# Gathered rows used one per tick at a group's end, with a sum over partitions moved among the last tiles

## Chip, cores and metric

The kernel runs on 1 core of one Trainium2 chip. The metric is the device time of one execution in microseconds (us); the kernel before takes 3470.04 us, the median of 3 runs (3468.87 to 3470.82).

## What is computed

One residual block on 512 tokens of width 2048 in fp32: a gated merge of forgetting attention and multi-scale pooling, and then PEER, a retrieval of experts of one neuron each. The change lies in the last part:

```python
q = (xt @ w_query)                                  # 8 heads
top 16 of 256 candidates per head -> expert_idx, gates = softmax(top_s)
def token_block(args):
    xb, idx, g = args
    u = jnp.take(expert_u, idx, axis=0)             # 128 rows of 2048 per token
    a = jnp.einsum('thkd,td->thk', u, xb)
    hid = jax.nn.gelu(a) * g
    vsel = jnp.take(expert_v, idx, axis=0)
    return jnp.einsum('thk,thkd->td', hid, vsel)
x = x + peer(rms_norm(x, norm2_g), ...)
```

## The kernel before, in words

The 512 tokens are treated in three parts. The first 128 (group 0 of the rows) and the last 64 (group 1 of the rows) fetch the rows of their experts, as the reference does. The 320 in the middle are multiplied with all 16384 experts, of which most get a gate of zero.

**Gathered rows.** A list `items` holds 128 fetches of `u` rows and 128 of `v` rows for group 0, then 64 and 64 for group 1, whose 64 tokens are spread over two partitions each (`GQ` = 2), so that the two halves have to be added in the end. A fetch (`row_load`, L787) is an indirect DMA of POOL's queue that brings one row of 2048 to each of 128 partitions, 1 MB, into one of two, later three buffers (`row`, `xrow`). Its use (`row_use`) is one instruction of VectorE (DVE): a dot product with `tok`, the tokens, for `u` (L824), and a multiply-add into `tok`, now the sum, for `v` (L827). Rows are doled out by `tick`, which stands in the middle of every tile of the products: first `run_gens` takes each generator of `gens` one step on, then `rows(rate)` adds `rate` to a credit (3 at most) and for every whole credit uses the oldest row and fetches another. While `hold` is set, a row that would have to be used waits. When all rows of a group are fetched, the last line of `rows` uses all that are still in the buffers, in that same tick. The use of the last `u` row starts `to_v`: it loads the tokens into `tok` once more (SP's queue), takes the Gelu on ScalarE (ACT) and one tick later multiplies with the gates and, for group 1, masks `tok`. The use of the last `v` row starts `to_next`: for group 0 it stores `tok` as `yg`, and then `tok_u` loads and scales the tokens of group 1.

**The joint stage.** The dense tokens go through 32 groups of 512 experts. In the first 16 only `u` is multiplied, and the result goes to memory; the other 16, the joint stage from about 2090 us on, have twelve tiles each: four U tiles (`u_tile`, 48 matmuls into `psm`) and eight V tiles (48 matmuls into `psv`, `s` = 0 to 7). Each weight tile is loaded by SP's queue (`wraw`, `xraw`, L152), rounded to a high half `whi` by ACT (L162), and the low half `wlo` is made by VectorE (L174), two pieces each, up to two tiles ahead; a matmul is done as three with high and low halves. `h_make` (L1440 to L1443) gates the activations of a U tile, `at`, or of a stored one, `sp`, and splits them into `h5h` and `h5l`, which the V tiles multiply. After a V tile VectorE adds `psv` to `acc` (L1498). Each of the 192 tiles holds one tick, with a `rate` of the rows left over 184. POOL, ACT, SP and VectorE take their instructions in the order in which the program issues them.

**The end.** After the last V tile, rows that are left are used; a 128 x 64 matrix `sel` of zeros and ones is built (L1508 to L1513), four matmuls with it add the two halves of each of the last 64 tokens (L1517), ACT copies each out of PSUM (L1518), and SP stores the result as `yg2` (L1519).

```python
    def rows(rate):
        ...
        if row["n"] == len(items) or items[row["n"]][0] != row["grp"]:
            while row["live"] and not row["hold"]:
                row_use()
```

Of the kernel before, what the change touches and what calls it, by code (L numbers as in the profile page):

```python
# [12 lines left out]
F32 = mybir.dt.float32  # L13
F32R = mybir.dt.float32r
I32 = mybir.dt.int32
# [3 lines left out]
OP = mybir.AluOpType  # L19
AX = mybir.AxisListType  # L20

P = 128
S = 512
# [11 lines left out]
NG = NB - ND  # L35
GQ = P // NG
# [26 lines left out]
def block_kernel(ctx, tc, a):  # L63
    nc = tc.nc
# [5 lines left out]
    prow = ctx.enter_context(tc.tile_pool(name="prow", bufs=1))  # L70
# [71 lines left out]
    def row_tile():  # L142
        extra["row"] += 1
        if extra["rows"] is not None and extra["row"] % 3 == 0:
            return extra["rows"].tile([P, D], F32, name="xrow")
        return prow.tile([P, D], F32, name="row", bufs=2)
# [55 lines left out]
    gens = []  # L202

    def run_gens():
        for g in list(gens):
            try:
                next(g)
            except StopIteration:
                gens.remove(g)
# [52 lines left out]
    def acc_bank():  # L262
        return psm.tile([P, S], F32, name="psm")
# [83 lines left out]
    for c in range(4):  # L347
        x4 = xA[:, 4 * c:4 * c + 4, :]
        nc.vector.tensor_tensor(x4, x4, g1[:, 4 * c:4 * c + 4, None].to_broadcast([P, 4, NA]),
                                op=OP.mult)  # L350
# [207 lines left out]
    for n, (kind, i) in enumerate(groups_a):  # L558
        ps = acc_bank()
# [127 lines left out]
    for i in range(4):  # L687
        ps = acc_bank() if i else first_o
# [11 lines left out]
    tok = prow.tile([P, D], F32, name="tok")  # L700
# [76 lines left out]
    row = dict(n=0, credit=0.0, live=[], hold=0, on=False, ready=0, grp=0)  # L777
# [21 lines left out]

    def to_v(grp, n):  # L800
        row["hold"] = 1
        src = x2t_d if grp == 0 else x2g_d.rearrange("t q d -> (t q) d")
        nc.sync.dma_start(tok, src)
        nc.scalar.activation(gact[:, :n], gact[:, :n], AF.Gelu_apprx_tanh)
        yield
        nc.vector.tensor_tensor(gact[:, :n], gact[:, :n], ggat[grp], op=OP.mult)
        if grp:
            nc.vector.tensor_scalar(tok, tok, qmask[:, 0:1], None, op0=OP.mult)
        row["hold"] = 0

    def to_next(grp):
        row["hold"] = 1
        if grp == 0:
            nc.sync.dma_start(a["yg"], tok)
            yield
            yield from tok_u(x2g_d.rearrange("t q d -> (t q) d"), rg[:, 0:1])
            row["hold"] = 0
            row["grp"] = 1
        yield

    def row_use():
        grp, kind, j, n, r = row["live"].pop(0)
        if kind == "u":
            nc.vector.scalar_tensor_tensor(r, r, 1.0, tok, op0=OP.mult, op1=OP.mult,  # L824
                                           accum_out=gact[:, j:j + 1])
        else:
            nc.vector.scalar_tensor_tensor(tok, r, gact[:, j:j + 1], tok, op0=OP.mult, op1=OP.add)  # L827
        if j == n - 1:
            gens.append(to_v(grp, n) if kind == "u" else to_next(grp))
            run_gens_last()  # L830

    def depth():
        return 2 if extra["rows"] is None else 3

    def rows(rate):
        if not row["on"]:
            return
        row["credit"] = min(row["credit"] + rate, 3.0)
        while row["credit"] >= 1.0 and row["n"] < len(items) and items[row["n"]][0] == row["grp"] \
                and row["grp"] < row["ready"]:  # L840
            if len(row["live"]) >= depth():
                if row["hold"]:
                    return
                row_use()
            if len(row["live"]) < depth():
                row_load()
            row["credit"] -= 1.0
        if row["n"] == len(items) or items[row["n"]][0] != row["grp"]:
            while row["live"] and not row["hold"]:
                row_use()  # L850

    def tick(rate):
        run_gens()
        rows(rate)
# [36 lines left out]
    for i in range(4):  # L891
        kk = p3.tile([P, 2, 2 * P], F32, name="kk", bufs=2)
        nc.gpsimd.dma_start(kk, a["keys"][2 * i:2 * i + 2].rearrange("h p i k -> p h (i k)"))
        ps = acc_bank()
# [166 lines left out]
    for n, (kind, i) in enumerate(order_b):  # L1061
        if n == len(order_b) - 7:
            extra["raws"] = extra["rows"] = None
        ps = acc_bank()
# [4 lines left out]
        elif kind == "pin":  # L1069
# [3 lines left out]
            if i == 7:  # L1073
                ps = acc_bank()
# [33 lines left out]
    for c in (2, 3, 0, 1):  # L1108
        rv = p2.tile([P, 4, NB], F32, name="apr", bufs=1)
        nc.sync.dma_start(rv, ap_d[c])  # L1110
        for j in range(4):
# [3 lines left out]
                                    op=OP.subtract)  # L1115
# [52 lines left out]
    for dt in range(KD):  # L1168
# [5 lines left out]
        ps = acc_bank()  # L1174
# [95 lines left out]
    for h in range(H):  # L1270
# [3 lines left out]
        for half in range(2):  # L1274
            if h == 0 and half == 0:
                ps = first_q
            else:
                ps = acc_bank()
# [167 lines left out]
    def h_later(hps, n, at, gt, i):  # L1446
        hps[n] = h_make(at, gt, i)
        yield

    left_rows = len(items) - row["n"]  # L1450
    ticks = 12 * (NIG - LAG)
    rate = left_rows / (ticks - 8)
    sps = {}

    def spilled(g, i):
# [10 lines left out]
    for g in range(LAG):  # L1466
# [11 lines left out]
        for s in range(8):  # L1478
# [8 lines left out]
            ps = psv.tile([P, 2, S], F32, name="psv")  # L1487
# [14 lines left out]
    while row["live"] or row["n"] < len(items):  # L1502
        run_gens()
        rows(2.0)
    run_gens()

    sel = prow.tile([P, NG], F32, name="selg")
    si = prow.tile([P, NG], I32, name="selgi")  # L1508
    nc.gpsimd.iota(si, pattern=[[-GQ, NG]], base=0, channel_multiplier=1)
    nc.vector.tensor_scalar(sel, si, 0.0, None, op0=OP.is_ge)  # L1510
    sel2 = prow.tile([P, NG], F32, name="selg2")
    nc.vector.tensor_scalar(sel2, si, float(GQ), None, op0=OP.is_lt)
    nc.vector.tensor_tensor(sel, sel, sel2, op=OP.mult)  # L1513
    out = row_tile()
    for c in range(4):
        ps = acc_bank()
        nc.tensor.matmul(ps[:NG], lhsT=sel, rhs=tok[:, c * S:(c + 1) * S], start=True, stop=True)  # L1517
        nc.scalar.copy(out[:NG, c * S:(c + 1) * S], ps[:NG])  # L1518
    nc.sync.dma_start(a["yg2"], out[:NG])  # L1519
    es_v.close()  # L1520
    es_7.close()
    es_6.close()
# [74 lines left out]
```

## Time and profile before

| what | value |
|---|---|
| median of 3 runs | 3470.04 us |
| the profiled execution, its time | 3467.64 us |
| its span, first to last instruction | 3465.8 us |
| busy: TensorE (PE), VectorE (DVE), ScalarE (ACT), GpSimd (POOL) | 96%, 77%, 44%, 19% |
| mean granted clock of TensorE | 0.985 |
| bytes moved | 1036.90 MB, 299 GB/s on the mean |

The busy share of TensorE comes from modelled ends of pipelined matmuls, so the waits and the granted clock say more than it does. Waits are given as the instruction that waited, what it waited for, the sum in us, the number of waits and the longest. In a timeline the first column is the start in us from the span's start, the second the length in us; what stands in brackets at the end is the idle time ahead and what ended it. The granted clock is a share of 2.4 GHz.

### The profile page before, as it was taken

What the parts mean: (1) busy time and instruction counts of PE and PEld (TensorE: products, weight loads), DVE (VectorE), ACT (ScalarE), POOL (GpSimd) and SP (SyncE); (2) the same over time, 40 slices, a digit from 0 to 9 for tenths busy, and PEclk for the clock granted to TensorE, in tenths of its full rate; (3) what the DMA queues carried; (4) which work ended last, traced back from release to release, by engine and by line L of the source; (5) the groups of instructions that cost most, each with busy time, mean ns of one, the idle gap of its engine ahead of it and who ended that gap; (6) DMA issues with size and microseconds to landing.
All of it is one profiled execution on the core that took longest, in us unless ns stands there. A gap on an engine that the chain in (4) does not pass through costs nothing.

```text
span 3465.8 us, 50471 instructions
## 1 busy us (share of the span) xinstructions
PE 3334.0 (96%) x20236; PEld 3155.4 (91%) x20236; DVE 2685.1 (77%) x3482; ACT 1515.4 (44%) x2263; POOL 652.4 (19%) x411
## 2 busy tenths in 40 slices
PE   7999899999998999999999989999999999999998
PEld 5656599999998999999999989999999999999997
DVE  5556787787876876887778758888887888888885
ACT  5655434545443333346476753333333333333332
POOL 0000012233321221310000002222222222222221
PEclk9999999999998999999999999999999999999999
DMA  7898867787877897864555689999998999899994
GB/s 263 305 360 313 312 239 272 268 312 268 309 288 283 319 362 278 312 229 161 201 189 193 215 305 345 357 355 351 350 347 338 359 354 354 338 358 353 340 357 151
DMA packets 226762, 1036.90 MB, mean 299 GB/s; under 512 B 21344, under 2 KB 107536, under 8 KB 112928
## 3 DMA queue, kind: packets, MB, share of 16 engines
q1 hardware_dynamic: 144640, 574.14, 44.4%
q0 software_dynamic: 56480, 406.96, 31.5%
q10 hardware_dynamic: 25408, 52.59, 3.9%
q8 instruction: 158, 2.59, 0.3%
q14 instruction: 76, 0.62, 0.0%
HBM read 980.05 MB, written 53.56 MB: 298 GB/s over the span
## 4 chain that ended last, share of the span: by engine, by line
PE 55%; DVE 14%; issue 12%; DMA 8%; ACT 7%; POOL 2%; ACTq 0%; SPq 0%; POOLq 0%; DVEq 0%
PE psm L223 9%; PE psm L221 9%; PE psm L222 9%; PE psv L222 6%; PE psv L223 6%; PE psv L221 6%; PE psm L240 6%; DVE wlo L174 5%; DMA row<-v,gidx 3%; ACT whi L162 3%; ACT o L1385 2%; DVE tok L827 1%; POOL row L787 1%; PE psx L222 1%; PE psx L223 1%
## 5 line engine op out<-in xcount | busy, mean ns | idle before, releaser
L174 DVE TENSOR_TENSOR wlo<-wraw,whi 128x1024 fp32r<-128x1024 f32 x728 | 869.2, 1220 | 294.9 <-ACT whi L162 291.6
L162 ACT CAST whi<-wraw 128x1024 fp32r<-128x1024 f32 x728 | 753.5, 1047 | 658.0 <-PE psv L222 375.9
L223 PE MATMUL psv<-h5h,wlo 128*128 128x320 f32 x2048 | 636.1, 311 | 14.3 <-DVE wlo L174 14.3
L221 PE MATMUL psm<-xnh,whi 128*128 128x320 f32 x2048 | 637.4, 311 | 10.3 <-ACT at L1410 9.8
L221 PE MATMUL psv<-h5h,whi 128*128 128x320 f32 x2048 | 636.7, 311 | 6.6 <-ACT h5h L1442 6.4
L223 PE MATMUL psm<-xnh,wlo 128*128 128x320 f32 x2048 | 634.3, 310 | 6.7 <-DVE wlo L174 6.6
L222 PE MATMUL psv<-h5l,whi 128*128 128x320 f32 x2048 | 637.4, 311 | 1.1
L222 PE MATMUL psm<-xnl,whi 128*128 128x320 f32 x2048 | 633.8, 309 | 0.0
L787 POOL DMA_INDIRECT row<-v,gidx x139 | 219.1, 1576 | 1136.4 <-DVE tok L827 1090.1
L223 PEld LDWEIGHTS psv<-h5h,wlo 128*128 128x128 f32 x2048 | 386.9, 189 | 15.3 <-DVE wlo L174 15.3
L221 PEld LDWEIGHTS psm<-xnh,whi 128*128 128x128 f32 x2048 | 386.5, 189 | 10.8 <-ACT at L1410 10.0
L221 PEld LDWEIGHTS psv<-h5h,whi 128*128 128x128 f32 x2048 | 387.0, 189 | 8.8 <-ACT h5h L1442 8.8
L223 PEld LDWEIGHTS psm<-xnh,wlo 128*128 128x128 f32 x2048 | 386.3, 189 | 8.1 <-DVE wlo L174 8.1
L222 PEld LDWEIGHTS psv<-h5l,whi 128*128 128x128 f32 x2048 | 386.9, 189 | 4.9 <-DVE h5l L1443 4.6
L222 PEld LDWEIGHTS psm<-xnl,whi 128*128 128x128 f32 x2048 | 386.5, 189 | 0.0
L221 PE MATMUL psm<-hh,whi 128*128 128x384 f32 x1024 | 353.6, 345 | 0.0
L787 POOL DMA_INDIRECT row<-u,gidx x135 | 223.8, 1658 | 660.1 <-DVE row L824 567.2
L222 PE MATMUL psm<-hl,whi 128*128 128x384 f32 x1024 | 346.4, 338 | 0.0
L223 PE MATMUL psm<-hh,wlo 128*128 128x384 f32 x1024 | 346.4, 338 | 0.0
L827 DVE SCALAR_TENSOR_TENSOR tok<-row,gact,tok 128x2048 f32<-128x2048 f32 x139 | 326.0, 2345 | 19.1 <-DMA row<-v,gidx 18.0
L824 DVE SCALAR_TENSOR_TENSOR row<-row,tok 128x2048 f32<-128x2048 f32 x135 | 307.4, 2284 | 9.1 <-DMA row<-u,gidx 9.0
L162 ACT CAST whi<-xraw 128x1024 fp32r<-128x1024 f32 x148 | 153.5, 1046 | 182.2 <-PE psv L222 145.7
(393 smaller groups left out, 5183.4 us busy)
## 6 DMA issues: line engine op xcount, KB each, us to landing
wraw<-uT SPq DMA_DIRECT2D x112, 1024.0 KB, 6.7
wraw<-vd SPq DMA_DIRECT2D x96, 1024.0 KB, 7.4
wraw<-w1A SPq DMA_DIRECT2D x48, 1024.0 KB, 6.7
xraw<-vd SPq DMA_DIRECT2D x32, 1024.0 KB, 9.4
wraw<-wgl SPq DMA_DIRECT2D x23, 1024.0 KB, 8.4
g_d<-stg ACTq DMA_DIRECT2D x10, 2048.0 KB, 10.9
gt<-g_d SPq DMA_DIRECT2D x32, 640.0 KB, 10.3
xraw<-w1A SPq DMA_DIRECT2D x16, 1024.0 KB, 7.3
```

The source lines that it names most:

```text
L162: nc.scalar.copy(hi, raws[i][:, half * HD:(half + 1) * HD])
L174: nc.vector.tensor_tensor(lo, raws[i][:, half * HD:(half + 1) * HD], hi.bitcast(F32), op=OP.subtract)
L221: nc.tensor.matmul(ps, lhsT=wh, rhs=xh, start=first and i == 0, stop=False)
L222: nc.tensor.matmul(ps, lhsT=wh, rhs=xl, start=False, stop=False)
L223: nc.tensor.matmul(ps, lhsT=wl, rhs=xh, start=False, stop=last and i == n - 1)
L240: nc.tensor.matmul(ps, lhsT=xs[:, k, :], rhs=ws, start=first and kk == 0 and n == 0, stop=last and kk == 3 and n == len(terms) - 1)
L787: nc.gpsimd.indirect_dma_start(out=r, out_offset=None, in_=a[kind], in_offset=bass.IndirectOffsetOnAxis(ap=gidx[grp][:, j:j + 1], axis=0))
L824: nc.vector.scalar_tensor_tensor(r, r, 1.0, tok, op0=OP.mult, op1=OP.mult, accum_out=gact[:, j:j + 1])
L827: nc.vector.scalar_tensor_tensor(tok, r, gact[:, j:j + 1], tok, op0=OP.mult, op1=OP.add)
L1385: nc.scalar.activation(o2[:, j, :], o2[:, j, :], AF.Copy, scale=idT[2][:, 4 * q + j:4 * q + j + 1])
```

## The change

Four things change. At the end of a group at most one row is used per tick, and none in a tick that has used one already (`used`). What follows a group's last use starts one tick later (`yield` after `hold` is set), and for group 0 the next `tok` is loaded another tick later. The sum over partitions goes into `to_next`, which spreads its four matmuls and copies over ticks of the last V tiles; its matrix is built ahead of the joint stage. The rate is the rows left over 180 ticks, in place of 184.

```diff
     def to_v(grp, n):
         row["hold"] = 1
+        yield
         src = x2t_d if grp == 0 else x2g_d.rearrange("t q d -> (t q) d")
         nc.sync.dma_start(tok, src)
         nc.scalar.activation(gact[:, :n], gact[:, :n], AF.Gelu_apprx_tanh)
...
     def to_next(grp):
         row["hold"] = 1
+        yield
         if grp == 0:
             nc.sync.dma_start(a["yg"], tok)
+            yield
             yield
             yield from tok_u(x2g_d.rearrange("t q d -> (t q) d"), rg[:, 0:1])
             row["hold"] = 0
             row["grp"] = 1
-        yield
+        else:
+
+            out = row_tile()
+            for c in range(4):
+                ps = acc_bank()
+                nc.tensor.matmul(ps[:NG], lhsT=selg[0], rhs=tok[:, c * S:(c + 1) * S],
+                                 start=True, stop=True)
+                yield
+                nc.scalar.copy(out[:NG, c * S:(c + 1) * S], ps[:NG])
+            nc.sync.dma_start(a["yg2"], out[:NG])
...
         row["credit"] = min(row["credit"] + rate, 3.0)
+        used = False
...
                 row_use()
+                used = True
...
         if row["n"] == len(items) or items[row["n"]][0] != row["grp"]:
-            while row["live"] and not row["hold"]:
+            if row["live"] and not row["hold"] and not used:
                 row_use()
...
     left_rows = len(items) - row["n"]
     ticks = 12 * (NIG - LAG)
-    rate = left_rows / (ticks - 8)
+    rate = left_rows / (ticks - 12)
...
     while row["live"] or row["n"] < len(items):
         run_gens()
         rows(2.0)
-    run_gens()
-
-    sel = prow.tile([P, NG], F32, name="selg")
...
-    out = row_tile()
-    for c in range(4):
-        ps = acc_bank()
-        nc.tensor.matmul(ps[:NG], lhsT=sel, rhs=tok[:, c * S:(c + 1) * S], start=True, stop=True)
-        nc.scalar.copy(out[:NG, c * S:(c + 1) * S], ps[:NG])
-    nc.sync.dma_start(a["yg2"], out[:NG])
+    while gens:
+        run_gens()
```

The six instructions that build `sel` stand unchanged ahead of `left_rows` now. Line numbers of the changed kernel differ: a use of a `u` row is L838, of a `v` row L841, the accumulation L1523.

Where the instructions move, on VectorE at the last V tiles of group 15. A row use is `tok<-row,gact,tok`, or with `xrow`. Before:

```order
L174 TENSOR_TENSOR wlo<-wraw,whi 128x1024 x2
L827 SCALAR_TENSOR_TENSOR tok<-row,gact,tok 128x2048
L827 SCALAR_TENSOR_TENSOR tok<-xrow,gact,tok 128x2048
L827 SCALAR_TENSOR_TENSOR tok<-row,gact,tok 128x2048 x2
L1498 TENSOR_TENSOR acc<-acc,psv 128x640
L174 TENSOR_TENSOR wlo<-wraw,whi 128x1024 x2
L1498 TENSOR_TENSOR acc<-acc,psv 128x640
L174 TENSOR_TENSOR wlo<-xraw,whi 128x1024 x2
L1498 TENSOR_TENSOR acc<-acc,psv 128x640
L174 TENSOR_TENSOR wlo<-wraw,whi 128x1024 x2
```

and with the change:

```order
L174 TENSOR_TENSOR wlo<-wraw,whi 128x1024 x2
L841 SCALAR_TENSOR_TENSOR tok<-row,gact,tok 128x2048
L1523 TENSOR_TENSOR acc<-acc,psv 128x640
L174 TENSOR_TENSOR wlo<-wraw,whi 128x1024 x2
L841 SCALAR_TENSOR_TENSOR tok<-row,gact,tok 128x2048
L1523 TENSOR_TENSOR acc<-acc,psv 128x640
L174 TENSOR_TENSOR wlo<-xraw,whi 128x1024 x2
L841 SCALAR_TENSOR_TENSOR tok<-xrow,gact,tok 128x2048
L1523 TENSOR_TENSOR acc<-acc,psv 128x640
L174 TENSOR_TENSOR wlo<-wraw,whi 128x1024 x2
L841 SCALAR_TENSOR_TENSOR tok<-row,gact,tok 128x2048
L1523 TENSOR_TENSOR acc<-acc,psv 128x640
```

The four uses in one tick are one use in each of the first five V tiles.

On SP's queue, where the rows of group 0 have ended, in group 6; `yg<-tok` is the store of the sum, `tok<-x2g_d` the load that overwrites it, `xrow<-g2r` the factors. Before:

```order
L152 DMA wraw<-vd 128x2048
L814 DMA yg<-tok 128x2048
L1434 DMA gt<-g_d 128x10x128
L152 DMA wraw<-vd 128x2048
L793 DMA tok<-x2g_d 128x2048
L795 DMA xrow<-g2r 128x2048
L1457 DMA sp<-a_d 128x320
L152 DMA xraw<-vd 128x2048
```

and with the change:

```order
L152 DMA wraw<-vd 128x2048
L1482 DMA sp<-a_d 128x320
L152 DMA xraw<-vd 128x2048
L816 DMA yg<-tok 128x2048
L1482 DMA sp<-a_d 128x320
L152 DMA wraw<-uT 128x2048
L1482 DMA sp<-a_d 128x320
L152 DMA wraw<-uT 128x2048
L793 DMA tok<-x2g_d 128x2048
L795 DMA xrow<-g2r 128x2048
```

The store and the loads stand later, behind other weight loads, and further from each other.

On VectorE in group 11, where the `u` rows of group 1 have ended; `gact<-gact,ggat` and `tok<-tok,qmask` are the gates and the mask of `to_v`. Before:

```order
L824 SCALAR_TENSOR_TENSOR row,gact<-row,tok 128x2048
L174 TENSOR_TENSOR wlo<-wraw,whi 128x1024 x2
L806 TENSOR_TENSOR gact<-gact,ggat_2302 128x64
L808 TENSOR_SCALAR tok<-tok,qmask 128x2048
L1440 TENSOR_TENSOR at<-at,gt 128x320
L1443 TENSOR_TENSOR h5l<-at,h5h 128x320
L1440 TENSOR_TENSOR sp<-sp,gt 128x320
L1443 TENSOR_TENSOR h5l<-sp,h5h 128x320
L827 SCALAR_TENSOR_TENSOR tok<-row,gact,tok 128x2048
L1440 TENSOR_TENSOR at<-at,gt 128x320
```

and with the change:

```order
L838 SCALAR_TENSOR_TENSOR row,gact<-row,tok 128x2048
L1523 TENSOR_TENSOR acc<-acc,psv 128x640
L174 TENSOR_TENSOR wlo<-wraw,whi 128x1024 x2
L1523 TENSOR_TENSOR acc<-acc,psv 128x640
L174 TENSOR_TENSOR wlo<-xraw,whi 128x1024 x2
L807 TENSOR_TENSOR gact<-gact,ggat_2302 128x64
L809 TENSOR_SCALAR tok<-tok,qmask 128x2048
L841 SCALAR_TENSOR_TENSOR tok<-row,gact,tok 128x2048
L841 SCALAR_TENSOR_TENSOR tok<-xrow,gact,tok 128x2048
L841 SCALAR_TENSOR_TENSOR tok<-row,gact,tok 128x2048
L1523 TENSOR_TENSOR acc<-acc,psv 128x640
L174 TENSOR_TENSOR wlo<-wraw,whi 128x1024 x2
```

The last use of a `u` row, the gates and the mask have moved from U tiles to V tiles; one tick without a row use stands between, and three uses follow the mask at once.

## Rows read from the trace of the kernel before

**Rows 1.** Waits of PE, whole run: line <- waited for: us, times, longest.

```profile
PE psv L223 <- DVE wlo L174: 14.3, 4, 7.9
```

**Rows 2.** Waits of PE at 2640:2690, 2690:3020, 3020:3060 and 3390:3415, in this order.

```profile
PE psv L223 <- DVE wlo L174: 6.4, 3, 5.0
...
PE psv L221 <- ACT h5h L1442: 0.3, 1, 0.3
...
PE psv L221 <- ACT h5h L1442: 2.7, 1, 2.7
...
PE psv L223 <- DVE wlo L174: 7.9, 1, 7.9
```

**Rows 3.** DVE timeline (start, us, ...): accumulations behind V tile 7, groups 0, 5, 6, 10, 11, 14, 15.

```profile
2156.70 0.82 DVE L1498 TENSOR_TENSOR acc<-acc,psv 128x640 f32<-128x640 f32 x1 [1.69 <-PE psv L223]
...
2581.28 0.82 DVE L1498 TENSOR_TENSOR acc<-acc,psv 128x640 f32<-128x640 f32 x1 [1.69 <-PE psv L223]
...
2676.09 0.81 DVE L1498 TENSOR_TENSOR acc<-acc,psv 128x640 f32<-128x640 f32 x1
...
3014.44 0.82 DVE L1498 TENSOR_TENSOR acc<-acc,psv 128x640 f32<-128x640 f32 x1 [1.74 <-PE psv L223]
...
3104.84 0.82 DVE L1498 TENSOR_TENSOR acc<-acc,psv 128x640 f32<-128x640 f32 x1 [1.69 <-PE psv L223]
...
3359.66 0.82 DVE L1498 TENSOR_TENSOR acc<-acc,psv 128x640 f32<-128x640 f32 x1 [1.08 <-PE psv L223]
...
3454.76 0.82 DVE L1498 TENSOR_TENSOR acc<-acc,psv 128x640 f32<-128x640 f32 x1 [6.22 <-PE psv L223]
```

**Rows 4.** Windows: us, busy and count by engine (PE PEld DVE ACT POOL), PEclk, DMA, GB/s.

```profile
2640.00:2650.00 10.00, 7.04 (x36) 7.05 (x37) 7.04 (x7) 0.00 (x0) 3.41 (x2) 0.67 0.82 292
3411.00:3415.00 4.00, 4.00 (x17) 4.00 (x18) 3.81 (x4) 0.00 (x0) 0.00 (x0) 0.54 0.99 341
```

**Rows 5.** DVE timeline, group 15: first and last of four row uses, and the low halves.

```profile
3395.88 2.34 DVE L827 SCALAR_TENSOR_TENSOR tok<-row,gact,tok 128x2048 f32<-128x2048 f32 x1
...
3406.46 2.35 DVE L827 SCALAR_TENSOR_TENSOR tok<-row,gact,tok 128x2048 f32<-128x2048 f32 x1 [3.45 <-DMA row<-v,gidx]
...
3409.46 2.35 DVE L174 TENSOR_TENSOR wlo<-wraw,whi 128x1024 fp32r<-128x1024 f32 x2
```

**Rows 6.** Timeline, group 6: SP's V weight behind the store of tok, and DVE's low halves.

```profile
2641.98 5.62 SPq L152 DMA_DIRECT2D wraw<-vd  x1
...
2658.41 2.36 DVE L174 TENSOR_TENSOR wlo<-wraw,whi 128x1024 fp32r<-128x1024 f32 x2 [5.92 <-ACT whi L162]
```

**Rows 7.** Timeline, group 11: ACT's Gelu of the rows, and DVE's mask.

```profile
3038.16 0.26 ACT L804 ACTIVATE gact<-gact 128x64 f32<-128x64 f32 x1 [2.77 <-DVE row L824]
...
3042.87 1.29 DVE L808 TENSOR_SCALAR tok<-tok,qmask 128x2048 f32<-128x2048 f32 x1 [0.85 <-DMA tok<-x2g_d]
```

**Rows 8.** Timeline of the end: an accumulation, the sum over partitions, its copies, the store.

```profile
3447.71 0.82 DVE L1498 TENSOR_TENSOR acc<-acc,psv 128x640 f32<-128x640 f32 x1 [3.95 <-PE psv L223]
...
3456.09 3.67 PE L1517 MATMUL psm<-tok,selg 128*64 128x512 f32 x8 [1.38 <-DVE selg L1513]
...
3457.20 0.58 ACT L1518 COPY xrow<-psm 64x512 f32<-64x512 f32 x1 [15.63 <-PE psm L1517]
...
3459.80 0.58 ACT L1518 COPY xrow<-psm 64x512 f32<-64x512 f32 x1 [0.28 <-PE psm L1517]
...
3460.41 0.55 SPq L1519 DMA_DIRECT2D yg<-xrow  x1
```

**Rows 9.** DVE timeline: first use of a v row, and the joint stage's start.

```profile
1359.38 2.35 DVE L827 SCALAR_TENSOR_TENSOR tok<-row,gact,tok 128x2048 f32<-128x2048 f32 x1 [7.17 <-DMA row<-v,gidx]
...
2078.71 2.50 DVE L174 TENSOR_TENSOR wlo<-wraw,whi 128x1024 fp32r<-128x1024 f32 x2 [13.58 <-ACT whi L162]
```

**Rows 10.** GB/s in 40 slices of the span (page, part 2), and the window 2670:2680.

```profile
GB/s 263 305 360 313 312 239 272 268 312 268 309 288 283 319 362 278 312 229 161 201 189 193 215 305 345 357 355 351 350 347 338 359 354 354 338 358 353 340 357 151
...
2670.00:2680.00 10.00, 10.00 (x70) 10.00 (x70) 9.57 (x11) 2.77 (x5) 1.88 (x2) 1.00 1.01 418
```

More of the change, by code (lines that the diff above doesn't have):

```diff
@@ L818, in to_next @@
             row["grp"] = 1
-        yield
+        else:
[7 more added lines that the diff above has]
+            nc.sync.dma_start(a["yg2"], out[:NG])
+    selg = []
     def row_use():
@@ L1448, in h_later @@
         yield
+    sel = prow.tile([P, NG], F32, name="selg")
+    si = prow.tile([P, NG], I32, name="selgi")
+    nc.gpsimd.iota(si, pattern=[[-GQ, NG]], base=0, channel_multiplier=1)
+    nc.vector.tensor_scalar(sel, si, 0.0, None, op0=OP.is_ge)
+    sel2 = prow.tile([P, NG], F32, name="selg2")
+    nc.vector.tensor_scalar(sel2, si, float(GQ), None, op0=OP.is_lt)
+    nc.vector.tensor_tensor(sel, sel, sel2, op=OP.mult)
+    selg.append(sel)
     left_rows = len(items) - row["n"]
     ticks = 12 * (NIG - LAG)
-    rate = left_rows / (ticks - 8)
+    rate = left_rows / (ticks - 12)
     sps = {}
@@ L1504, in block_kernel @@
         rows(2.0)
-    run_gens()
-    sel = prow.tile([P, NG], F32, name="selg")
[L1508 to L1513, printed above, removed]
-    out = row_tile()
-    for c in range(4):
-        ps = acc_bank()
-        nc.tensor.matmul(ps[:NG], lhsT=sel, rhs=tok[:, c * S:(c + 1) * S], start=True, stop=True)
-        nc.scalar.copy(out[:NG, c * S:(c + 1) * S], ps[:NG])
-    nc.sync.dma_start(a["yg2"], out[:NG])
+    while gens:
+        run_gens()
     es_v.close()
```

## Prediction

> **What bounds the kernel now.** I read the waits of TensorE first, then the starts of one VectorE line to see which stretches are longer than their like, then the instructions around each long stretch, and last the tail and the transfer rates.
>
> The reader is to see that in the joint stage (16 groups of four U tiles and eight V tiles) TensorE is the bound, and that it is let down at a few places only. Over the whole run it waits 14.3 us for the low halves of V tiles (`psv` for `wlo`), in four waits [rows 1]; 6.4 us of them lie at 2640 to 2690 us, 7.9 at 3390 to 3415, and at 3020 to 3060 there are 2.7 us more for `h5h` [rows 2]. These are the places where gathered rows change group or kind, or run out: group 6 (rows of the first 128 tokens end), group 11 (`u` to `v` rows of the last 64), group 15 (the end).
>
> A wait costs more than itself. The starts of the accumulation behind V tile 7 show it [rows 3]: five undisturbed groups take (2581.28 - 2156.70)/5 = 84.92 us each. Group 6 takes 94.81 (9.89 over), group 11 90.40 (5.48 over), group 15 95.10 (10.18 over): 25.55 us in all, against some 17 us of listed waits. Part of the rest is the clock: after TensorE has idled for the 7.9 us its granted clock is 0.54 in the next 4 us, and it is 0.67 at 2640 to 2650, so mostly at 1.2 GHz in the one and part of the time in the other, against 2.4 GHz else [rows 4].
>
> The causes stand in the same stretches. In group 15 four row uses are issued in one tick; they start at 3395.88, the last waits 3.45 us for its row and starts at 3406.46, and only behind it come the accumulation and the low halves at 3409.46, which TensorE has been waiting for [rows 5]. In group 6 the same happens, and the store of `tok`, issued in that tick, stands on SP's queue ahead of weight loads until the last use is done: the next V weight is issued at 2641.98 (its issue alone spans 5.62 us), and `wlo` at 2658.41 has waited 5.92 us for `whi` [rows 6]. In group 11 ACT's Gelu, issued in the tick of the last `u` use, holds ACT for 2.77 us, then the mask waits 0.85 us for `tok` [rows 7].
>
> **The change, part by part.** The sum is made against the profiled execution, 3467.64 us; the median of the runs, 3470.04, is 2.40 above it, which I add at the end.
>
> *One row per tick at a group's end, the follow-up a tick later.* Group 6: after the change this group has no tick with more than two row uses in the order, the store of `tok` goes out one tick after its last use (so SP never waits there) and the next `tok` two ticks on. The product that opens the next rows falls alone in a tick of the next group's U tiles. VectorE then has less per tick than in any undisturbed tick, so I take the whole excess as gained: 9.89 us; bounds 0 and 9.89. Group 15: one use in each of V tiles 0 to 4, none waiting for a fresh fetch, since three buffers at one use per 7.05 us tick leave some 21 us for a fetch that took under 11 here (it could go out only behind the use of 3395.88, and was there at 3406.46): 10.18 us gained; bounds 5 and 10.18.
>
> Group 11: Gelu and the mask move into V tiles. What is late next is one tick with the mask and three row uses, 1.29 + 3 x 2.35 = 8.34 us on VectorE [rows 5, 7]. Queued behind it are the accumulation and the low halves of the tile after next. Where VectorE has caught up, which the empty tick ahead of it gives, a V tile's start is followed by the accumulation (0.82) and two halves (2.35), then the burst, then accumulation and the first half of the tile after next: 3.17 + 8.34 + 0.82 + 1.18 = 13.5 us, against two tiles of 7.05 (3447.71 to 3454.76) on TensorE, 14.1 [rows 3, 5, 8]. It fits by 0.6 us if `tok` has landed; the wait seen now, 0.85, would use that up. I take 0.5 us lost of the 5.48 gained; bounds: nothing lost, or all 5.48 lost again.
>
> *The higher rate* (rows left over 180 ticks in place of 184). By the order the pairs (two uses in a tick) are 42 in place of 40, and come on the fourth U tile in seven groups (0 to 2, 12 to 15) in place of four. That is the worst place: `h5h` of that tile is needed in the next tile. Group 0 is the same before and after; of the other three pairs in that place one costs TensorE 0.3 us and two nothing [rows 2]. Three more at 0.3: 0.9 us lost; bounds 0 and 3 x 2.35 = 7.
>
> *The sum over partitions among the last V tiles.* Each of the four products with its pieces takes (3459.80 - 3457.20)/3 = 0.87 us on TensorE [rows 8]. Three now stand between V tiles, on the path: 2.6 us lost. They wait for nothing: `tok` is final a tick earlier, and the copies on ACT, 0.58 us each, lie in its idle time. The tail gets shorter. Now from the last accumulation (3454.76) to the issue of the last store (3460.41) it is 5.65 us; after, one product (3456.09 to 3457.20, 1.11) and one copy with the way to SP's issue (3459.80 to 3460.41, 0.61) are left, 1.7 us: 3.9 us gained; bounds 3 and 4.1. Store and end behind it stay.
>
> *The selection matrix, built early.* Three instructions of VectorE and one of POOL go to the start of the joint stage, into 13.58 us in which VectorE waits anyway [rows 9]: nothing. If POOL, whose row fetch stands ahead, came late there, it would cost what this cover can't hold, some 1 us.
>
> *The change from `u` to `v` rows of the first tokens.* VectorE waits 7.17 us for a row at 1359 [rows 9], and TensorE for nothing in that stretch. Nothing, within plus or minus 4 us.
>
> Sum: -25.55 + 0.5 + 0.9 + 2.6 - 3.9 = -25.45 us; 3467.64 - 25.45 = 3442.2; with the 2.40 of the median **3444.6 us**, 0.73% faster. About 0.2% (6.9 us) is what a measurement of this kernel can tell from no change.
>
> **Rivals.** *A new wait in place of the old ones.* If the burst in group 11 costs all of its 5.48 again and the pairs their 7, of which I have counted 0.5 and 0.9, 11 us go: 3455.7. For it: VectorE has no idle tick around U tiles. Against it: pairs have cost 0.3 so far.
>
> *The transfers bound it.* A shorter stage moves the same rows in less time. Slices 26 to 30 of the span, groups without a long wait, move 347 to 357 GB/s, 352 on the mean [rows 10]; rows, about half of these bytes (some 15 of 1 MB a group beside 12 weight tiles of that size), at a 2% higher rate ask for some 356. If 352 were the limit, a group would take 1.1% longer, 0.97 us, over 15 groups 14.5: 3459. If 347 were, 2.6%, 2.2 us a group, 33 us: 3478. Against it: 418 GB/s were moved at 2670 to 2680 [rows 10], and no row is waited for between the places named. The Trainium skill (DMA: Bandwidth & Descriptors, "Where 436 GB/s comes from") puts what HBM gives one core at about 358 GB/s and says that this side binds loads from HBM. By that limit 356 would pass with almost nothing to spare, and the catch-up after a pause would not, so it speaks for this rival; the 418 measured here goes against it.
>
> *Slower: VectorE becomes the bound in U tiles.* Fourteen groups have a pair in a U tile after the change. If each made TensorE wait its 2.35 us and lose 2 us to the clock besides (half of the 4 us stretch of [rows 4]), 14 x 4.35 = 61 us: 3505. It decides from 2.4 us per pair on: 14 x 2.4 = 33, the gain and 6.9 more. Against it: the order before has thirteen such pairs, and outside groups 0 and 11 they show 0.3 us in all.
>
> *The change doesn't do what it says*: the waits only move by a tick, since a fetch still comes late. Then groups 6 and 15 keep their excess, and only group 11, the pairs and the tail are left: 3470.04 - 4.98 + 0.9 - 1.3 = 3464.7, no change. Against it stand the empty ticks in the order.
>
> **How the numbers follow.** Forecast 0.78; new wait 0.10; transfers 0.05 (0.02 faster, 0.02 no change, 0.01 slower); no effect 0.04; VectorE bound 0.03. Faster 0.78 + 0.10 + 0.02 = 0.90, the same 0.02 + 0.04 = 0.06, slower 0.01 + 0.03 = 0.04. The range takes in the bounds around the forecast (nothing lost at the burst and pairs, 4 us at the first change of rows: 3439) and the first rival: **3438 to 3457 us**.
>
> **What would show it.** Right: no wait of TensorE for `wlo` over 1 us after 2600 us; groups 6 and 11 at 84.9 to 86 us, group 15 at 87.5; the granted clock at 1.00 through the last three; four products of `tok`, three of them between V tiles; last store under 2 us after the last accumulation. Wrong: a wait of several us behind the burst in group 11, waits for `h5h` in groups 1, 2 and 12 to 15, or row uses that wait for their fetches in mid-group.

## The result, and the profile after

The changed kernel takes 3448.68 us (median of 6 runs, 3445.58 to 3456.2), the kernel before 3469.56 (6 runs beside them, 3468.15 to 3470.86): ratio 0.9943, 95% interval 0.9931 to 0.9955. The forecast was 3444.6, its range 3438 to 3457. The profiled execution took 3448.07 us, with a span of 3446.3.

TensorE's waits from the joint stage on come first. For its products all of 2120 to 3480 us lists one wait, at 3072 us, in group 11 (the waits of its weight loads have a list of their own, which comes up at e_urate):

```profile
PE psv L223 <- DVE wlo L174: 1.3, 1, 1.3
```

The waits of groups 6 and 15 [rows 2] are gone. The accumulations behind V tile 7 of groups 0, 5, 6, 10, 11, 14 and 15 answer to [rows 3] (VectorE's timeline: start, duration, instruction, idle time before it):

```profile
2161.62 0.81 DVE L1523 TENSOR_TENSOR acc<-acc,psv 128x640 f32<-128x640 f32 x1
...
2584.93 0.82 DVE L1523 TENSOR_TENSOR acc<-acc,psv 128x640 f32<-128x640 f32 x1 [1.69 <-PE psv L223]
...
2669.47 0.82 DVE L1523 TENSOR_TENSOR acc<-acc,psv 128x640 f32<-128x640 f32 x1 [3.95 <-PE psv L223]
...
3008.50 0.82 DVE L1523 TENSOR_TENSOR acc<-acc,psv 128x640 f32<-128x640 f32 x1 [1.74 <-PE psv L223]
...
3095.57 0.81 DVE L1523 TENSOR_TENSOR acc<-acc,psv 128x640 f32<-128x640 f32 x1
...
3351.11 0.81 DVE L1523 TENSOR_TENSOR acc<-acc,psv 128x640 f32<-128x640 f32 x1
3414.55 0.82 DVE L1523 TENSOR_TENSOR acc<-acc,psv 128x640 f32<-128x640 f32 x1 [1.69 <-PE psv L223]
3422.78 0.82 DVE L1523 TENSOR_TENSOR acc<-acc,psv 128x640 f32<-128x640 f32 x1 [5.14 <-PE psv L223]
...
3439.25 0.82 DVE L1523 TENSOR_TENSOR acc<-acc,psv 128x640 f32<-128x640 f32 x1 [7.41 <-PE psv L223]
```

From the two traces the whole span is accounted for:

| stretch (us) | before | after | foretold | measured |
|---|---|---|---|---|
| up to group 0's last accumulation | 2156.70 | 2161.62 | 0 (±4) | +4.92 |
| group 6 | 94.81 | 84.54 | -9.89 | -10.27 |
| group 11 | 90.40 | 87.07 | -4.98 | -3.33 |
| group 15, three products in it | 95.10 | 88.14 | -7.58 | -6.96 |
| the twelve other groups | 1017.75 | 1017.88 | +0.9 | +0.13 |
| last accumulation to the end of the span | 11.04 | 7.05 | -3.9 | -3.99 |
| span | 3465.8 | 3446.3 | -25.45 | -19.5 |

Below the first line it is -24.42, one us from the sum. Two lines need an explanation: group 11 still takes more than its neighbours, and each V tile with a product takes 3422.78 - 3414.55 = 8.23 us where one without takes 7.04.

In group 11 the burst of mask and three uses runs as foretold (VectorE; below it POOL's issues of the rows that refill the three buffers):

```profile
3054.26 1.28 DVE L809 TENSOR_SCALAR tok<-tok,qmask 128x2048 f32<-128x2048 f32 x1
3055.57 2.35 DVE L841 SCALAR_TENSOR_TENSOR tok<-row,gact,tok 128x2048 f32<-128x2048 f32 x1
...
3060.35 2.35 DVE L841 SCALAR_TENSOR_TENSOR tok<-row,gact,tok 128x2048 f32<-128x2048 f32 x1
...
3069.55 2.35 DVE L841 SCALAR_TENSOR_TENSOR tok<-row,gact,tok 128x2048 f32<-128x2048 f32 x1 [3.85 <-DMA row<-v,gidx]
```

```profile
3058.19 2.93 POOL L787 DMA_INDIRECT row<-v,gidx  x1 [10.29 <-DVE tok L841]
3061.43 2.08 POOL L787 DMA_INDIRECT xrow<-v,gidx  x1 [0.30 <-issue]
3063.82 1.56 POOL L787 DMA_INDIRECT row<-v,gidx  x1 [0.30 <-issue]
```

What waits is not the burst but the use a tick later: three uses in one tick empty all three buffers, so the next row, asked for at 3058.19, is not there until 3069.55, 11.4 us later. An accumulation and the next low halves stand behind that use. The tail answers to [rows 8]: ACT's last copy and SP's store.

```profile
3440.25 0.58 ACT L830 COPY xrow<-psm 64x512 f32<-64x512 f32 x1 [4.13 <-PE psm L827]
...
3440.86 0.55 SPq L831 DMA_DIRECT2D yg<-xrow  x1
```

The store is issued 1.6 us after the last accumulation starts, 5.65 before.

### The profile page after: what moved, and what is told of

The parts are those of the page before. It is cut to its first block, busy times and chain, and to the rows that moved or that the text cites. A ratio compares the mean times of both kernels' runs of the same rounds, so it can differ in the third digit from the quotient of the medians.

```text
span 3446.3 us, 50478 instructions
## 1 busy us (share of the span) xinstructions
PE 3331.0 (97%) x20236; PEld 3151.2 (91%) x20236; DVE 2684.6 (78%) x3482; ACT 1516.3 (44%) x2263; POOL 659.1 (19%) x411
## 4 chain that ended last, share of the span: by engine, by line
PE 58%; DVE 17%; issue 8%; DMA 8%; ACT 7%; POOL 1%; ACTq 0%; SPq 0%; DVEq 0%; POOLq 0%
PE psm L223 9%; PE psm L222 9%; PE psm L221 9%; PE psv L222 6%; PE psv L223 6%; PE psv L221 6%; DVE wlo L174 6%; PE psm L240 6%; DVE tok L841 3%; DMA row<-v,gidx 2%; ACT whi L162 2%; ACT o L1401 1%; PE psx L1382 1%; DMA wraw<-wquA 1%; PE psx L222 1%
## 5 line engine op out<-in xcount | busy, mean ns | idle before, releaser
L787 POOL DMA_INDIRECT row<-v,gidx x139 | 232.6, 1674 | 1128.0 <-DVE tok L841 1085.1
L841 DVE SCALAR_TENSOR_TENSOR tok<-row,gact,tok 128x2048 f32<-128x2048 f32 x139 | 326.0, 2345 | 10.2 <-DMA row<-v,gidx 9.3
L838 DVE SCALAR_TENSOR_TENSOR row<-row,tok 128x2048 f32<-128x2048 f32 x135 | 307.4, 2284 | 13.5 <-DMA row<-u,gidx 13.4
```

Source lines behind the costliest of these rows:

```text
L787: nc.gpsimd.indirect_dma_start(out=r, out_offset=None, in_=a[kind], in_offset=bass.IndirectOffsetOnAxis(ap=gidx[grp][:, j:j + 1], axis=0))
```

## The experiments

Start, stage and tail are of the profiled execution: the start of group 0's last accumulation, from there to the last accumulation, and from that to the end of the span.

| kernel | median us (runs) | ratio to before, 95% | start | groups 6 / 11 / 15 | stage | tail |
|---|---|---|---|---|---|---|
| before | 3469.56 (6) | | 2156.70 | 94.81 / 90.40 / 95.10 | 1298.06 | 11.04 |
| after | 3448.68 (6) | 0.9943 (0.9931 to 0.9955) | 2161.62 | 84.54 / 87.07 / 88.14 | 1277.63 | 7.05 |
| after_again | 3450.99 (5) | 0.9952 (0.9939 to 0.9966) | 2158.65 | 84.57 / 89.06 / 88.15 | 1279.74 | 7.01 |
| e_drain | 3471.90 (10) | 1.0003 (0.9994 to 1.0013) | 2163.78 | 96.81 / 89.27 / 100.84 | 1303.74 | 4.18 |
| e_noyield | 3451.94 (4) | 0.9946 (0.9929 to 0.9963) | 2161.96 | 84.57 / 89.44 / 94.31 | 1284.79 | 4.15 |
| p_drain | 3445.50 (4) | 0.9931 (0.9914 to 0.9947) | 2160.06 | 84.56 / 84.87 / 85.18 | 1272.09 | 11.05 |
| e_credit | 3452.10 (4) | 0.9946 (0.9930 to 0.9963) | 2163.04 | 84.57 / 84.86 / 88.76 | 1279.01 | 7.05 |
| e_sum_end | 3444.86 (4) | 0.9930 (0.9914 to 0.9947) | 2157.90 | 84.57 / 87.60 / 84.57 | 1274.68 | 9.62 |
| e_sum_one | 3448.26 (4) | 0.9938 (0.9921 to 0.9955) | 2165.41 | 84.57 / 87.54 / 88.37 | 1278.45 | 4.14 |
| e_f32r | 3441.19 (4) | 0.9922 (0.9905 to 0.9939) | 2157.00 | 84.57 / 86.76 / 87.31 | 1276.61 | 4.19 |
| e_best2 | 3443.42 (4) | 0.9922 (0.9904 to 0.9940) | 2163.32 | 85.20 / 84.86 / 87.94 | 1278.63 | 4.15 |
| e_urate | 3440.45 (5) | 0.9920 (0.9907 to 0.9934) | 2156.00 | 84.47 / 85.89 / 87.44 | 1271.18 | 7.02 |
| e_top | 3434.31 (4) | 0.9897 (0.9882 to 0.9912) | 2157.25 | 84.48 / 90.35 / 86.30 | 1272.87 | 4.18 |
| e_top2 | 3433.32 (4) | 0.9894 (0.9878 to 0.9911) | 2158.39 | 84.47 / 83.45 / 86.31 | 1268.94 | 4.17 |

The start spreads over 9 us, 2156.00 to 2165.41, though all have the same order up to the first change from `u` to `v` rows. The spread is there before anything that was changed can act. VectorE's first use of a gathered row, in the kernel before and in the changed one:

```profile
488.37 2.29 DVE L824 SCALAR_TENSOR_TENSOR row<-row,tok 128x2048 f32<-128x2048 f32 x1 [1.76 <-DMA row<-u,gidx]
493.25 2.29 DVE L838 SCALAR_TENSOR_TENSOR row<-row,tok 128x2048 f32<-128x2048 f32 x1 [2.47 <-DMA row<-u,gidx]
```

These are 4.88 us apart, of the 4.92 at the start of the joint stage. Most medians are of four to six runs and carry that spread; stage and tail don't, so the small effects are read from these. Stage and tail are of one execution each, and the repeat below says how far they can be trusted.

**The changed kernel again.**

> The changed kernel once more, for two questions. Theory (what the profiles differ by ahead of the joint stage, 2156.7 to 2165.4 us at the first group's last accumulation over ten profiles with one order there, comes and goes with the execution): the start of the joint stage falls anywhere in these 9 us, and its groups take the same times again within 0.3 us each, 87.1 for group 11 and 88.1 for group 15 among them. Rival (each program has its own start, by where its parts lie in memory): 2161 to 2162 again.

The start came 3 us earlier than in the first profile of the same kernel: the theory. The groups repeat within 0.03 us, but for group 11, which took 89.06 (its late row was waited for 4.31 us, not 3.85). What is left there is thus 2.2 to 4.1 us over the 84.92 of an undisturbed group. Three more profiles below have the same order there (e_sum_end, e_sum_one, e_f32r) and take 86.76 to 87.60, so between kernels of that order a difference of 1 or 2 us in group 11 says little.

**What made the waits: e_drain.** `if row["live"] and not row["hold"] and not used:` is `while row["live"] and not row["hold"]:` again.

> The changed kernel, but a group's end is drained again in one go (five row uses in one tick in group 6, four in group 15, where they fall in the third U tile); the follow-up a tick later and the sum among the V tiles are kept. Theory (the drain made the waits): group 6 again 6 to 10 us over 84.9, group 15 again 6 to 10 us over its 88.1; in all 12 to 20 us more, 3461 to 3469 us. Rival (the follow-up issued in the tick of the last use made them: the store of tok on SP, Gelu on ACT): both groups stay as in the changed kernel, 3447 to 3451 us.

All of the gain is lost, and more stage time than foretold. TensorE's waits at 2120 to 3480:

```profile
PE psv L223 <- DVE wlo L174: 10.5, 1, 10.5
PE psm L827 <- DVE tok L841: 10.0, 1, 10.0
PE psv L221 <- ACT h5h L1458: 3.0, 1, 3.0
```

The first is group 6, for the reason of [rows 5]: the last use waits for a row just asked for. The second I had not priced: the first product of the sum stands on TensorE a tick after the drain and waits for it. The third is group 11, where Gelu, mask and three uses fall in U tiles here.

**e_noyield.** The first `yield` of `to_v` and of `to_next` and the second one behind the store of `tok` are left out.

> The changed kernel, but what follows a group is issued in the tick of its last use again, as in the kernel before; one use per tick and the sum among the V tiles are kept. Theory (the drain made the waits, and the follow-up only let them grow): SP and ACT now wait for one use of 2.35 us, not for four: group 6 at 84.9 to 87, group 11 at 85 to 88, 3447 to 3453 us. Rival (the follow-up's place made the waits): group 6 again some 9.9 over, group 11 some 5.5 over, about 3464 us.

Group 6 needs none of them: 84.57. Group 15 loses 6.2 us against the changed kernel, 1.2 of it for a fourth product between V tiles, the rest since the first product is issued in the tick of the last use and waits for `tok` (the first row below, 3395 to 3415), with what follows the wait. Group 11 takes 89.44, over the 85 to 88 expected, and 0.4 to 2.4 more than in the two profiles of the changed kernel: the rows change in the third U tile here, where Gelu on ACT delays `h5h` (the second, 3010 to 3050) as in the kernel before [rows 2, 7].

```profile
PE psm L824 <- DVE tok L838: 2.7, 1, 2.7
...
PE psv L221 <- ACT h5h L1455: 2.8, 1, 2.8
```

**One part alone: p_drain.** The kernel before with `used` and the `if`, nothing else.

> The kernel before with one part of the change alone: at a group's end one row use per tick. The follow-up stays in the tick of the last use, the sum and its matrix at the end, the rate as before. Theory (this part alone carries the gain): group 6 at 84.6 to 85 us in place of 94.81, group 15 at 84.6 to 87 in place of 95.10, group 11 at 85 to 89 in place of 90.40, the tail from the last accumulation 11.0 us as before or up to 3 longer (the last row is used one tile later): 3447 to 3453 us. Rival (the yields or the other rate are needed too): group 6 or 15 keeps half of its excess or more: 3457 us or later.

This part alone brings all of it, and the median lies below the range expected: its stage is 5.5 us shorter than the changed kernel's, its whole 1.5 shorter by stage and tail. Group 11 is at 84.87 with the follow-up in the tick of the last use. The rows change in a V tile here and one use follows the mask; where the rows change falls out of the count of ticks. The load of `tok` was issued at 3051.34, 4.9 us ahead of the mask:

```profile
3056.19 1.29 DVE L808 TENSOR_SCALAR tok<-tok,qmask 128x2048 f32<-128x2048 f32 x1 [1.12 <-DMA tok<-x2g_d]
3057.51 2.35 DVE L827 SCALAR_TENSOR_TENSOR tok<-row,gact,tok 128x2048 f32<-128x2048 f32 x1
...
3062.79 2.34 DVE L827 SCALAR_TENSOR_TENSOR tok<-xrow,gact,tok 128x2048 f32<-128x2048 f32 x1
```

**The three uses behind the mask: e_credit.** `row["credit"] = 0.0` behind `row["hold"] = 0` in `to_v`, and `ticks - 14`.

> The changed kernel, but when a group's hold ends the credit is set to 0, and the rate is the rows left over 178 ticks in place of 180, so that the rows end in the same tick; one use stands behind the mask of group 11 in place of three, and 47 pairs in place of 42. Theory (what is left in group 11 is that three buffers are freed together and refetched at once, so that the next use waits 3.85 us for its row): no wait of that row over 1 us, no wait of TensorE for wlo there, group 11 at 84.9 to 85.3 in place of 87.07; about 2 us less, 3446 to 3447 us. Rival (it is the mask and the Gelu in the V tiles, or the pairs, whatever the burst): group 11 stays at 86.5 to 87.5, and five more pairs cost 0 to 1.5 us: 3448.5 to 3450 us.

Group 11 is at 84.86, as the theory has it, but the stage is 1.4 longer: group 8 takes 86.78, with two pairs among its four U tiles and this wait of TensorE, the only one listed for its products in the stage:

```profile
PE psv L221 <- ACT h5h L1459: 1.3, 1, 1.3
```

**Where the sum stands: e_sum_end.** The `else` of `to_next` is left out, and the four products with their copies follow the joint loop.

> The changed kernel, but the sum over partitions stands behind the joint loop as before (the selection matrix stays built early). From the changed kernel's trace: group 15 gives back the three inserted products (3 x 1.19 = 3.6 us, so 84.6 in place of 88.1), and from the last accumulation to the last store's issue it is 5.65 us again, not 1.6: 4.0 us more. Theory (the move gains next to nothing): 0.4 us more, 3448 to 3450 us. Rival (the products between V tiles lie beside idle TensorE time, so that moving them is worth the whole tail): 4 us more, 3452.7 us.

Group 15 gives back 3.57 us, the tail takes 2.57 more, not 4.0: moving the products costs 1.0 us. The 1.4 between this tail (9.62) and the one of before (11.04) is the early selection matrix, for which TensorE waited in [rows 8] (1.38). Neither the theory nor the rival had that. The median, 3.8 us below the changed kernel's, can't show 1.0 beside a start that was 3.7 earlier in the profile.

**All products in one tick: e_sum_one.** The `yield` between them is left out.

> The changed kernel with all four products of the sum in one tick, in the sixth V tile of group 15, in place of one per tick in three V tiles and one behind the last. Theory (each change between the float32 product and the float32r ones of the V tiles costs about 0.3 us, the product itself 0.87): this V tile takes 7.04 + 4 x 0.87 + 0.32 = 10.8 us, the two others 7.04, group 15 88.4. Rival (a product costs 1.19 wherever it stands): 7.04 + 4 x 1.19 = 11.8 us, group 15 89.4. In both the tail from the last accumulation to the span's end is that of the store of the accumulators, 4.2 us in place of 7.05, so that the time is 2 to 3 us less than that of the changed kernel by the same start of the joint stage.

The V tile with all four (VectorE's accumulations, then TensorE's products):

```profile
3418.95 0.82 DVE L1522 TENSOR_TENSOR acc<-acc,psv 128x640 f32<-128x640 f32 x1 [1.69 <-PE psv L223]
3429.78 0.82 DVE L1522 TENSOR_TENSOR acc<-acc,psv 128x640 f32<-128x640 f32 x1 [7.75 <-PE psv L223]
```

```profile
3422.36 3.67 PE L827 MATMUL psm<-tok,selg 128*64 128x512 f32 x8
```

10.83 us is 3.79 over 7.04, four products at 0.87 and 0.31 once; at 1.19 each it would be 11.8. So a visit to the float32 product costs 0.3 us beside the product, and the changed kernel makes three between V tiles.

**Products of another kind: e_f32r.** `hi = copy(tok)` and `lo = tok - hi` in float32r, eight products on a float32r selection matrix in the last V tile, then the copies and the store.

> The changed kernel with the sum done otherwise: tok is split into a float32r part and its rest (two ACT copies, two VectorE subtractions, in the seventh V tile, where both engines have time), and eight float32r products stand in the last V tile, with all four copies behind them and the store ahead of the last accumulation. Theory (a float32r product takes a quarter of a float32 one, and no kind is changed): 8 x 0.22 = 1.8 us on TensorE in place of 3.6, group 15 at 86.4 in place of 88.14, tail 4.2 us in place of 7.05: 4.6 us less by the same start of the joint stage. Rival (what the inserted products cost is their place in the middle of a V tile, not their kind): 8 products with as much overhead each as now, 0.3 us, group 15 at 88.8; then 2.2 us less.

Group 15 takes 0.9 us more than foretold and 2.74 more than without products (84.57), 0.7 of it a wait for a copy out of the same accumulator tile; stage and tail together are 3.9 less than the changed kernel's. The products follow each other at 0.23 us:

```profile
3427.14 0.40 PE L837 MATMUL psm<-whi,selgr 128*64 128x512 f32 x1
3427.37 0.39 PE L838 MATMUL psm<-wlo,selgr 128*64 128x512 f32 x1
...
3429.39 0.44 PE L837 MATMUL psv<-whi,selgr 128*64 128x512 f32 x1 [0.71 <-ACT xrow L839]
```

**The first combination: e_best2.** The sum of e_f32r, one tick earlier, and `row["credit"] = min(row["credit"], 1.0)` behind `row["hold"] = 0` in `to_v`.

> The float32r sum as in the run before it, and the credit capped at 1 when a group's hold ends, at the changed kernel's rate: two uses behind the mask of group 11 in place of three, 43 pairs, none of them in a fourth U tile and no two in one group's U tiles. Theory (three buffers refetched at once make the wait in group 11, two pairs in one group's U tiles made the 1.9 us of group 8 in the run with credit 0): group 11 at 84.9 to 85.5, no group but 15 over 85.5, group 15 at 86.4, tail 4.2: 6.5 us less than the changed kernel by the same start of the joint stage, about 3442 us. Rival (two freed together are enough to make the next row late): group 11 at 86.5 or more.

Group 11 is right again: two uses leave one row in its buffer. The rest isn't: groups 1 to 6, with a pair in the second U tile, took 85.20 each, group 15 took 87.94 in place of 86.4, and together they ate the gain.

**Pairs: e_urate.** `u_tile(at, 1.0, ...)`, and `rate = (12 * left_rows / (ticks - 14) - 4) / 8` for V tiles.

> The changed kernel with the credit raised by 1.0 in a tick of a U tile and by more in one of a V tile (12 ticks together as the rows left over 178 ticks): all pairs of row uses stand in V tiles, 42 as before. Theory (a pair in the last U tile of a group costs TensorE 0.6 us without a wait long enough to be listed: in the changed kernel groups 1, 2, 12, 13 and 14 with such a pair take 85.18 us, those with it in the first U tile 84.55): groups 1 to 5 and 12 to 14 at 84.5 to 84.6; from the first group's last accumulation to the last one 3 to 4 us less than 1277.6; group 11 unchanged at 87 (three uses behind the mask still). Rival (the 0.6 comes from elsewhere, the weights' loads or the spilled tiles): these groups keep 85.2, stage 1277 to 1278.

The stage is 6.45 shorter. 1.2 of it is in group 11, which moves by more than that from execution to execution. The others give 5.3, more than foretold: not only groups with a pair in the last U tile get shorter (85.18), those with one in the second do too (groups 8 to 10, from a mean of 84.85 to 84.34). In the changed kernel the windows of group 2 (pair in the last U tile) and group 5 (in the first) have the same products and no listed wait of them, 0.65 us apart; group 12 stands below for its last column (us, then busy time and count of PE, PEld, DVE, ACT and POOL, PEclk, DMA, GB/s):

```profile
2246.80:2332.00 85.20, 85.02 (x578) 84.54 (x577) 75.02 (x65) 29.68 (x37) 24.66 (x16) 1.00 0.93 357
2500.38:2584.93 84.55, 84.55 (x578) 84.48 (x577) 74.90 (x64) 29.35 (x37) 23.79 (x15) 1.00 0.94 359
...
3095.57:3180.75 85.18, 85.01 (x578) 84.52 (x577) 74.91 (x64) 29.66 (x37) 23.68 (x16) 1.00 0.96 366
```

The modelled busy time of the products (PE) all but hides the loss, and it shows in the weight loads (PEld). In group 2 they wait for the activations of the last U tile, whose gating (`at<-at,gt`) VectorE starts only behind the pair, which it runs from 2273.52 on (VectorE, then TensorE's weight loads):

```profile
2275.89 2.35 DVE L841 SCALAR_TENSOR_TENSOR tok<-row,gact,tok 128x2048 f32<-128x2048 f32 x1
2278.16 0.49 DVE L1456 TENSOR_TENSOR at<-at,gt 128x320 f32<-128x320 f32 x1
```

```profile
2279.20 0.19 PEld L221 LDWEIGHTS psv<-h5h,whi 128*128 128x128 f32 x1 [0.32 <-ACT h5h L1458]
2279.72 0.19 PEld L222 LDWEIGHTS psv<-h5l,whi 128*128 128x128 f32 x1 [0.34 <-DVE h5l L1459]
```

The list of the waits of weight loads (PEld) at 2165 to 3420 us has them, for the kernel before and for the changed one; before, 2.9 of the 4.8 us is the Gelu of group 11:

```profile
PEld psv L221 <- ACT h5h L1442: 4.8, 8, 2.9
PEld psv L222 <- DVE h5l L1443: 3.9, 14, 0.3
```

```profile
PEld psv L222 <- DVE h5l L1459: 3.1, 10, 0.3
PEld psv L221 <- ACT h5h L1458: 2.0, 6, 0.3
```

In the changed kernel the ten waits for `h5l` are one each in the ten groups from 1 on with a pair in the second, third or last U tile, the six for `h5h` in the six with a pair in the last. In e_urate and e_top2 neither is left.

**All together: e_top, e_top2.** e_top has U tiles at 1.0 (the rate for 180 ticks), the sum of e_f32r one tick earlier and with a bank for each of the last two, and no first `yield` in `to_v`. e_top2 has that `yield` and the cap at 1.0.

> All that the runs point to, together: one use per tick at a group's end, what follows the u rows in the tick of their last use again (so that one use stands behind the mask, not three), pairs in V tiles alone, the selection matrix early, and the sum with float32r products in the last V tile, each of the last two into a bank of its own. Theory (the costs seen are apart and add up): 14 groups at 84.55 and group 15 at 86.5, stage 1270, tail 4.2: 10 us less than the changed kernel by the same start, about 3438 us (3434 to 3442). Rival (pairs pressed into V tiles and the mask there make VectorE late in V tiles): group 11 or the groups with four pairs at 86 or more, and no more than 4 us are gained.

The median is 14.4 us below the changed kernel's, but group 11 fell to the rival, by a cause that it didn't name: without the empty tick the mask waits for its load of `tok` (VectorE), and TensorE for the low halves. That load was issued at 3044.82 and the mask could start 10.3 us later; p_drain, without an empty tick as well, had it in 4.9 and its mask waited 1.12. Why the load took twice as long here no run shows.

```profile
3055.11 1.29 DVE L808 TENSOR_SCALAR tok<-tok,qmask 128x2048 f32<-128x2048 f32 x1 [6.55 <-DMA tok<-x2g_d]
```

```profile
PE psv L223 <- DVE wlo L174: 2.8, 1, 2.8
```

> The run before with two things mended in group 11: what follows the u rows is issued a tick later again, as in the changed kernel (without that, the mask waited 6.55 us for its load of tok in the run before, and TensorE 2.8 us for wlo), and the credit is capped at 1 when the hold ends, so that two uses stand behind the mask, not three. Theory (the load of tok needs the empty tick, and two uses behind the mask cost nothing when a tick with one use follows): no wait of VectorE for tok over 1 us, groups 11 and 12 together 169 us in place of 173.5, stage 1268 to 1269, about 4.5 us less than the run before: 3430 us (3426 to 3434). Rival (the empty tick moves the wait to the rows behind it, as in the changed kernel): group 11 at 86.5 or more, no more than 2.5 us less than the run before.

No wait of TensorE's products is listed from 2120 us on, and from group 12 to 14 (3088 to 3341 us) products and weight loads are busy throughout, at 361 GB/s (columns as under e_urate):

```profile
3088.01:3341.02 253.01, 253.01 (x1727) 253.01 (x1727) 224.05 (x190) 88.79 (x109) 64.84 (x46) 1.00 0.94 361
```

Groups 1 to 14 average 84.47 us and group 15 takes 86.31. It is 0.45% faster than the changed kernel by the medians, with intervals against before that don't meet. Against e_top the stage is 3.9 us shorter; the medians, 1.0 apart, don't separate the two.

## Why the prediction was right, and where it was off

- *What bounds it.* Right: TensorE, let down where rows change or run out. e_drain against the changed kernel and p_drain against the one before show that the drain in one tick made the waits.
- *Group 6 and group 15.* Right within 0.4 us each (group 15 with its products taken off: 84.57 in e_sum_end). The store of `tok` on SP, to which I gave part of group 6, needs no yield once the drain is gone (e_noyield). Both gained a little more than foretold, since the 84.92 that I called undisturbed holds the loss at pairs: without pairs in U tiles a group takes 84.47 (e_top2).
- *Group 11.* The step that failed: "I take 0.5 us lost of the 5.48 gained". 2.15 us were lost, 4.1 in the repeat. I laid VectorE's burst against TensorE's two V tiles, and it fits; I didn't ask how many rows the burst leaves in the buffers. In group 15 I had counted three buffers at one use per tick against a fetch of under 11 us; three uses in one tick leave the next one a tick of 7. Nor is the gain the yield's: p_drain has all of it without. It goes with the place at which the rows change, a V tile in p_drain (84.87) and a U tile in e_noyield (89.44), both without the yield; no part of the change aims at a tile, so that they change in a V tile is luck. The yield gives `tok` more time to land, which e_top needed and p_drain didn't.
- *The higher rate.* 0.9 foretold, 0.13 measured, and the nearness is luck. "Three more at 0.3" is wrong: a pair behind the first U tile costs 0.4 to 0.7 us, in the kernel before as well (13 against 14 such pairs), so the two sums nearly cancel. I had read only the waits of the products, 0.3 us [rows 2]; the list of the weight loads has 5.1 us for the changed kernel, and e_urate gives 5.3 back.
- *The sum among the V tiles.* The term mis-sized: three products at 0.87 are 2.6, measured 3.57, since each also costs a change of kind. The tail came as foretold (-3.99 for -3.9), but 1.4 of that is the wait for the matrix, which its early building takes away and not the move of the products; I had put the matrix at nothing in its own step. The products' move alone costs 1.0 us.
- *Ahead of the joint stage.* The 4.92 us are not the change's: the order is the same up to 1342 us, and 4.88 are there at the first row use, at 490 us. The two profiles of the changed kernel differ by 3.0.
- *Transfers.* Not the bound. Group 12 moved 366 GB/s over 85 us, and e_top2 moved 361 over 253 us while TensorE waited for nothing. The Trainium skill (DMA: Bandwidth & Descriptors, "Where 436 GB/s comes from") puts the limit of what HBM gives one core at about 358 GB/s. The 366 lies above it, as did the 418 of [rows 10], and the measurement decides.
- *The signs I had named.* Of those for "right", the clock (1.00 in all three groups), the four products and the last store (1.6 us) came; the wait for `wlo` (1.3 us), group 11 (87.07) and group 15 (88.14) missed, and group 6 (84.54) came out lower still. Of those for "wrong" two came: a row use that waited 3.85 us for its fetch, and waits for `h5h` in groups 1, 2 and 12 to 15, too short for the list that I read.

The range held; the median came out 4.1 above the forecast. One us is in the terms above. The rest is no larger than the spread of the start, so how near the median came is partly luck.

## What to carry over

Where one engine feeds another tile by tile, spread side work at one piece per tile to the very end, and count for each burst how many buffers it leaves full, not only whether the burst fits. Put side work where the feeding engine has slack per tile (V tiles here), even if the list of the products' waits shows nothing, and read the waits of weight loads too, and the lengths of stretches that should be alike. When a change has several parts, run each alone: here one part carried the whole gain, and the changed kernel with its other parts took 1.5 us more by stage and tail.

## What the runs showed of the hardware

- A float32 product between float32r products costs 0.3 us beside its 0.87 (8.23 to 7.04 us a tile; 10.83 with four in a row); eight float32r products of the same columns took 1.8 us in all (86.31 to 84.47), four float32 ones 3.8.
- POOL's issue of a row fetch took longer beside VectorE. Of the 211 that start at 2160 to 3440 us in the changed kernel, 90 took 0.9 us, none of them beside a row use; 65 took 1.6 to 1.7, beside low halves for most or all of that time; 40 took 2.7 to 2.9, all beside a row use. The three behind the burst of group 11 took 2.93, 2.08 and 1.56.
- The first row use, behind one order of instructions, ended anywhere within 8.8 us over the fourteen profiles, at 490.59 to 499.38 us.
